# Interleaving TensorE transposes with products in a GLA and attention encoder

## The chip, the cores and the metric

The kernel runs on one core of one Trainium2 chip. The metric is the device time of one execution in microseconds (us); less is better. The executions shown below are of the kernel as it stood before the change.

## The reference

The reference is an encoder of two layers over 512 tokens of width 1024, in float32. Each layer is a token mixer and a gated MLP, each behind an RMS norm and with a residual:

```python
x = x + mixer(rmsnorm(x, norm_mix[i]))
x = x + conv_ffn(rmsnorm(x, norm_ffn[i]), ...)      # silu(gate) * val, width-3 convolution ahead
```

Layer 0 mixes by gated linear attention (GLA): 4 heads, keys of 128, values of 256 columns, chunks of 64, a scan in each direction. Its end is what the change touches:

```python
o = (o_f + o_b)                                     # per head: 512 tokens x 256
o = rmsnorm(o, norm_w) * silu(g)                    # the gated output
x = x + o.reshape(512, 1024) @ w_out
```

Layer 1 mixes by softmax attention: 8 query heads of 128, 2 key heads, 512 keys, swept in blocks of 128 queries:

```python
s = (q_blk @ k.T) * scale
p = softmax(s)                                      # 128 queries x 512 keys
o = p @ v                                           # then o.reshape(512, 1024) @ w_out
```

## The kernel before, in words

**Tiling.** Activations stand feature-major: 8 tiles of 128 features x 512 tokens. To keep float32's accuracy with operands of type `float32r`, every operand of a large product is split into a high part and a low part (what is left over), and one product becomes three matmuls into one accumulator: high by high, high by low, low by high (`mm3`, recorded at L350, L351, L352). A split takes one ScalarE copy (the high part) and one VectorE subtraction (the low part). Nearly every matmul moves 512 columns against a loaded 128x128 block.

**Stages.** In order: the GLA mixer (to about 205 us), MLP 0, attention (its block loop runs at about 628 to 727 us), MLP 1. Engines: PE does matmuls and transposes, DVE is VectorE, ACT is ScalarE, POOL is GpSimd; PEld are PE's weight loads. PSUM accumulators come from four pools of banks: `acc` 3, `s` 2, `pt` 2, `po` 1.

**Transposes.** Two results stand token-major and must be turned before they can be multiplied on. A transpose is a PE instruction on a 128x128 block, in groups of eight:
- `tail(h)` (L692 to L705) turns the gated output `gr` of GLA head `h`: for each of two column halves, four transposes into a `pt` bank (L699), then ACT copies it out with a scale as the high part of `oT` (L703) and DVE makes the low part (L704). Four heads, 32 transposes.
- `turn(h, i)` (L1094 to L1108) turns the probabilities of two query blocks: for each of two halves four transposes into a `pt` bank (L1105), then ACT (`pth`, L1107) and DVE (`ptl`, L1108). 16 calls, 128 transposes.

**GLA's heads.** Per head: scores inside the chunk (`inner`, L609), masked and split on ACT and DVE (`masked`: `at`, `ath`, `atl`, L616 to L622); state products (`kv`, `outer`), scanned on DVE into `sa` and `sb` (L655); the inner products with the values (L665) and with the states (`outputs`, L676). `gated(h)` then squares the output on ACT (L684), takes a power on POOL (L284), multiplies by the gate on DVE (L689, four instructions) and copies to `gr` by a DMA on POOL's queue (L690). `out_steps` (L408) is the output projection, cut into steps of six products; its first part works on the heads that are finished while the last head is still under way.

**Attention's loop.** Step `t` of the loop issues the scores of block `t` (three products, `s`), their maximum on DVE (`mx`, L1069), its scaling on ACT (`nb`, L1070), the exponential on ACT (`p`, L1072), and on DVE the reciprocal and the scaling (`rc`, L1077; `p`, L1078). ACT's queue then copies the block by DMA into a ring (L1090), from where it is turned five blocks later. `mix(h, k)` is the product with the values: three products per key block into the one `po` bank; after the fourth key block ACT and DVE split it into `oT` (L989, L990). The scores rotate over three banks. Query projections (`A`, `B`) and steps of the output projection (`op`) fill the rest of PE's time by two tables (`Q_STEPS`, `O_STEPS`).

**What sets the order.** The program is traced in Python; a scheduler then orders each engine's instructions by priority and by when it believes them ready, and adds the waits. Each engine issues its list strictly in that order. `with tc.issue_after(ins)` keeps what is traced inside it behind `ins` on the same engine. In the kernel before, attention's transposes and `mix` products have no such order; GLA's tails of heads 0 and 1 stand behind the head's last product:

```python
if h:
    tail(h - 1, last)                               # L744
with tc.issue_after(last.ins):
    last = qproj(h + 1, kqt)
```

and in attention, per step:

```python
for k in range(k, k + 1 if h < QH - 1 else NT):
    mix(h, k)                                       # L1141
if t >= LAG + 1 and (t - LAG) % 2 == 1 and t < len(blocks) + LAG:
    h, j = blocks[t - LAG]
    turn(h, j // 2)                                 # L1144
```

## Time and profile before

| | us |
|---|---|
| three executions | 1113.39, 1113.46, 1114.41 (median 1113.46) |
| profiled execution, its own time | 1113.35 |
| its span (first to last instruction) | 1111.6 |
| PE busy | 1104.1 (99%) |
| PE weight loads | 947.5 (85%) |
| DVE busy | 796.7 (72%) |
| ACT busy | 562.4 (51%) |
| POOL busy | 117.3 (11%) |
| granted TensorE clock | 0.999 |

The time contains 1.75 us outside the span. Matmuls are pipelined and their ends are modelled, so a product of 512 columns shows 0.39 us although products follow each other every 0.227 us; what a stretch costs PE is read from starts. A timeline row gives start, length, engine, line, operation, output <- inputs, shapes, count and, in brackets, the idle time before it with what ended it. A row with a count merges instructions that follow each other.

### The profile page before, as it was taken

To read this page: it belongs to the slowest core of one execution; us is meant where nothing else is said; L and a number is where in the kernel's file an instruction comes from. 1 tells how busy PE (TensorE), PEld (TensorE's weight loads), DVE (VectorE), ACT (ScalarE), POOL (GpSimd) and SP (SyncE) were. 2 spreads that over 40 slices of the span, in tenths; PEclk is the share of its full clock that TensorE was granted. 3 is DMA by queue.
4 is the path that set the end of the run, shared out by engine and by line. 5 is a ranking of instruction groups with operands and counts; after the bars stand their busy time and mean duration, and the time that the engine had idled before them with its cause. 6 is when DMAs were issued, how large, how long until landed. Compare 5 with 4: busy or idle time off the path is not lost.

```text
span 1111.6 us, 14744 instructions
## 1 busy us (share of the span) xinstructions
PE 1104.1 (99%) x5780; PEld 947.5 (85%) x5780; DVE 796.7 (72%) x1217; ACT 562.4 (51%) x870; POOL 117.3 (11%) x126
## 2 busy tenths in 40 slices
PE   9999999999999999999999999999999999999998
PEld 7888888888889988898888888788888998889887
DVE  6786784667889577975664588666788957797572
ACT  6565343444556444653464777644455644465340
POOL 0100122001001000100004333000100100010000
PEclk9999999999999999999999999999999999999999
DMA  6423122232226423363247665423222652336322
GB/s 230 152 76 112 59 95 77 76 114 76 76 88 177 155 76 113 102 165 114 97 130 186 174 191 161 143 76 108 82 76 82 172 164 76 114 96 167 117 76 76
DMA packets 31413, 130.52 MB, mean 117 GB/s; under 512 B 3824, under 2 KB 4336, under 8 KB 20976
## 3 DMA queue, kind: packets, MB, share of 16 engines
q1 hardware_dynamic: 21072, 102.16, 26.4%
q0 software_dynamic: 5376, 18.88, 8.5%
q10 hardware_dynamic: 4896, 8.55, 2.1%
q8 instruction: 45, 0.74, 0.3%
q14 instruction: 24, 0.20, 0.0%
HBM read 100.21 MB, written 2.10 MB: 92 GB/s over the span
## 4 chain that ended last, share of the span: by engine, by line
PE 96%; DVE 1%; issue 1%; ACT 1%; DMA 0%; POOL 0%; ACTq 0%; DVEq 0%; POOLq 0%
PE r L847 14%; PE up L350 14%; PE up L351 14%; PE up L352 14%; PE vg L382 8%; PE op L408 8%; PE dn L351 2%; PE dn L352 2%; PE dn L350 2%; PE A L350 1%; PE A L352 1%; PE A L351 1%; PE B L350 1%; PE B L351 1%; PE B L352 1%
## 5 line engine op out<-in xcount | busy, mean ns | idle before, releaser
L350 PE MATMUL up<-xhl,wh 128*128 128x512 f32 x704 | 274.4, 390 | 0.0
L351 PE MATMUL up<-xhl,wh 128*128 128x512 f32 x704 | 274.0, 389 | 0.0
L352 PE MATMUL up<-xhl,wl 128*128 128x512 f32 x704 | 273.9, 389 | 0.0
L199 ACT ACTIVATE wh<-raw 128x1024 fp32r<-128x1024 f32 x132 | 139.4, 1056 | 211.4 <-PE up L351 108.0
L200 DVE TENSOR_TENSOR wl<-raw,wh 128x1024 fp32r<-128x1024 f32 x132 | 161.1, 1220 | 41.2 <-ACT wh L199 40.9
L352 PEld LDWEIGHTS up<-xhl,wl 128*128 128x128 f32 x704 | 132.1, 188 | 27.5
L350 PEld LDWEIGHTS up<-xhl,wh 128*128 128x128 f32 x704 | 132.2, 188 | 27.1
L351 PEld LDWEIGHTS up<-xhl,wh 128*128 128x128 f32 x704 | 132.2, 188 | 27.0
L847 PE MATMUL r<-gu,wh 128*128 128x256 f32 x640 | 116.4, 282 | 0.0
L847 PEld LDWEIGHTS r<-gu,wh 128*128 128x128 f32 x640 | 99.7, 191 | 0.3
L789 DVE TENSOR_TENSOR u<-up,R 128x512 f32<-128x512 f32 x88 | 60.1, 685 | 54.0 <-PE up L352 54.0
L847 PE MATMUL r<-gu,wl 128*128 128x256 f32 x320 | 90.4, 283 | 0.0
L791 ACT ACTIVATE y<-u,cw 128x512 f32<-128x512 f32 x88 | 71.2, 811 | 33.1 <-DVE u L789 32.9
L382 PE MATMUL vg<-wh,xhl 128*128 128x512 f32 x256 | 79.7, 390 | 0.5 <-ACT sq L324 0.5
L408 PE MATMUL op<-oT,wh 128*128 128x512 f32 x256 | 71.8, 393 | 0.3 <-DVE g L689 0.3
L793 DVE SCALAR_TENSOR_TENSOR y<-u,cw,y 128x511 f32<-128x511 f32 x88 | 65.7, 748 | 2.0
L792 DVE SCALAR_TENSOR_TENSOR y<-u,cw,y 128x511 f32<-128x511 f32 x88 | 65.4, 744 | 1.2 <-ACT y L791 1.2
L795 ACT ACTIVATE y<-y 128x512 f32<-128x512 f32 x44 | 27.8, 633 | 72.0 <-DVE y L793 71.8
L847 PEld LDWEIGHTS r<-gu,wl 128*128 128x128 f32 x320 | 61.1, 191 | 0.0
L189 POOL DMA_DIRECT2D wl<-raw x32 | 28.1, 878 | 303.4 <-ACT wl L142 103.0
L382 PEld LDWEIGHTS vg<-wh,xhl 128*128 128x128 f32 x256 | 48.0, 188 | 10.6 <-ACT sq L324 0.7
L408 PEld LDWEIGHTS op<-oT,wh 128*128 128x128 f32 x256 | 47.3, 188 | 10.5 <-ACT oT L703 0.7
(232 smaller groups left out, 1928.3 us busy)
## 6 DMA issues: line engine op xcount, KB each, us to landing
raw<-in_w_up_dram SPq DMA_DIRECT2D x42, 1024.0 KB, 4.9
raw<-in_w_down_dram SPq DMA_DIRECT2D x22, 1024.0 KB, 4.8
wl<-raw POOLq DMA_DIRECT2D x32, 512.0 KB, 4.6
raw<-in_w_vg_dram SPq DMA_DIRECT2D x6, 1024.0 KB, 4.9
ring<-p ACTq DMA_DIRECT2D x22, 256.0 KB, 2.6
raw<-in_w_kq_dram SPq DMA_DIRECT2D x4, 1024.0 KB, 4.9
raw<-in_w_gout_dram SPq DMA_DIRECT2D x4, 1024.0 KB, 4.8
raw<-in_w_aout_dram SPq DMA_DIRECT2D x16, 256.0 KB, 4.5
```

Source lines behind the costliest of these rows:

```text
L199: act.activation(hi[:, sl], r[:, sl], AF.Copy)
L200: dve.tensor_tensor(lo[:, sl], r[:, sl], hi[:, sl].bitcast(F32), ALU.subtract)
L350: mm(ps, wh, mh, start=start, stop=False)
L351: mm(ps, wh, ml, start=False, stop=False)
L352: return mm(ps, wl, mh, start=False, stop=stop)
L382: mm(ps[j][:, :width], hl[k][i == 2][:, j * P : (j + 1) * P], (wl if i == 1 else wh)[:, sl], start=k == 0 and i == 0, stop=k == KC - 1 and ...
L408: mm(pss[ng][n], wt[:, sl], mv, start=k == 0 and i == 0, stop=k == KC - 1 and i == 2)
L789: dve.tensor_tensor(u, ps, norm.R, ALU.mult)
L791: act.activation(y, u, AF.Identity, scale=w(1), bias=w(3))
L792: dve.scalar_tensor_tensor(y[:, 1:], u[:, : S - 1], w(0), y[:, 1:], ALU.mult, ALU.add)
L793: dve.scalar_tensor_tensor(y[:, : S - 1], u[:, 1:], w(2), y[:, : S - 1], ALU.mult, ALU.add)
L847: mm(dst, w[:, sl], m, start=start and j == 0 and a == 0, stop=j == NQ - 1 and a == 2, skip_group_check=True)
```

## The change

Four edits; the products, the splits and the number of instructions stay.

1. `tail` and `turn` become generators that yield after two transposes and after each bank's copies. `behind` issues a PE instruction after the latest one of the same chain.
2. In GLA, the transposes of heads 0 and 1 are drawn between the steps (three products each) of the next head's query projection, those of heads 2 and 3 between the steps (six products) of the output projection. Its first part is now cut as four, two and two steps per column group instead of six and two, and from its third step on the products are chained in program order.
3. In the attention loop, `mix` yields after each of its three products, and each is chained; a pair of transposes is drawn ahead of each of them and ahead of its end. A step's chain starts behind the chain of the step before. The split of `po` is now traced behind the fourth pair.
4. For the last GLA head, `gated(2)` multiplies by the gate only after the low part `atl` of that head's masked scores.

```diff
--- before.py
+++ after.py
@@ -76,7 +76,18 @@
 ):
     nc = tc.nc
     pe, act, dve, pool, sync = nc.tensor, nc.scalar, nc.vector, nc.gpsimd, nc.sync
-    mm = pe.matmul
+    latest, chained = [None, None], [False]
+
+    def mm(*a, **k):
+        with tc.issue_after(latest[0].ins) if chained[0] else ExitStack():
+            latest[0] = pe.matmul(*a, **k)
+        return latest[0]
+
+    def behind(f, *a, **k):
+
+        with tc.issue_after(latest[0].ins) if latest[0] else ExitStack():
+            latest[0] = f(*a, **k)
+
 
     cp = ctx.enter_context(tc.tile_pool(name="cp", bufs=1))
     sp = ctx.enter_context(tc.tile_pool(name="sp", bufs=1))
@@ -554,9 +565,10 @@
                 pass
             return res
 
-        def qproj(h, kqt):
+        def qproj(h, kqt, beside=iter(())):
             psq = bank("acc" if h else "pt", "q")
-            last = feature_tile(*W.half(w_kq, 2 * h + 1), norm.hl, psq)
+            for last in feature_steps(*W.half(w_kq, 2 * h + 1), norm.hl, psq):
+                next(beside, None)
             dve.scalar_tensor_tensor(kqt[:, :S], psq, DK ** -0.5, norm.R, ALU.mult, ALU.mult)
             return last
 
@@ -619,8 +631,8 @@
             dve.copy_predicated(at3, msk, banks[1].rearrange("p (s c) -> p s c", c=P))
             hi, lo = f32r("u", "ath"), f32r("u", "atl")
             act.activation(hi, at, AF.Copy)
-            dve.tensor_tensor(lo, at, hi.bitcast(F32), ALU.subtract)
-            return hi, lo
+            on_dve = dve.tensor_tensor(lo, at, hi.bitcast(F32), ALU.subtract)
+            return hi, lo, on_dve
 
         def values(h):
 
@@ -676,7 +688,7 @@
                         last = mm(og[s], l, r, start=False, stop=i == len(parts) - 1, skip_group_check=True)
             return last
 
-        def gated(h, og):
+        def gated(h, og, after=None):
 
             oss = tiny(4, "oss")
             for s in range(NT):
@@ -686,23 +698,26 @@
             gr[h] = big(F32R, "gr")
             for s in range(NT):
                 r = g[s][:, h * DV : (h + 1) * DV]
-                dve.scalar_tensor_tensor(r, og[s], ors[:, s : s + 1], r, ALU.mult, ALU.mult)
+                with tc.issue_after(after.ins) if after else ExitStack():
+                    dve.scalar_tensor_tensor(r, og[s], ors[:, s : s + 1], r, ALU.mult, ALU.mult)
                 pool.dma_start(gr[h][:, s * DV : (s + 1) * DV].bitcast(F32), r)
 
-        def tail(h, last=None):
+        def tail(h):
 
             t3 = gr.pop(h)
             for c in range(2):
                 tp = bank("pt", "tp")
                 for s in range(NT):
-                    with tc.issue_after(last.ins) if last else ExitStack():
-                        pe.transpose(tp[:, s * P : (s + 1) * P].bitcast(F32R),
-                                     t3[:, s * DV + c * P : s * DV + (c + 1) * P], identr)
+                    behind(pe.transpose, tp[:, s * P : (s + 1) * P].bitcast(F32R),
+                           t3[:, s * DV + c * P : s * DV + (c + 1) * P], identr)
+                    if s == 1:
+                        yield
                 t = big(F32R, "oT") if h < 2 else pair("xhl", 8, F32R, "oT")
                 w = prm[:, PC_GN + c : PC_GN + c + 1]
                 act.activation(t[:, :S], tp, AF.Copy, scale=w)
                 dve.scalar_tensor_tensor(t[:, S:], tp, w, t[:, :S].bitcast(F32), ALU.mult, ALU.subtract)
                 oh[2 * h + c] = (t[:, :S], t[:, S:])
+                yield
 
         _, kqt = whole(kproj(0))
         ends, on_dve = keys(0, kqt)
@@ -733,7 +748,7 @@
                 last = outputs(h - 1, st, og, last)
                 banks, last = inner(h, last)
                 at = masked(banks)
-                gated(h - 1, og)
+                gated(h - 1, og, at[2])
             with tc.issue_after(on_act.ins) if h == 0 else ExitStack():
                 with tc.issue_after(on_dve.ins) if h == 0 else ExitStack():
                     vs = values(h)
@@ -741,19 +756,22 @@
             if h + 1 < GH:
                 with tc.issue_after(on_dve.ins):
                     ends, on_dve = keys(h + 1, kqt)
-                if h:
-                    tail(h - 1, last)
                 with tc.issue_after(last.ins):
-                    last = qproj(h + 1, kqt)
+                    last = qproj(h + 1, kqt, tail(h - 1) if h else iter(()))
         last = outputs(GH - 1, st, og, last)
         gated(GH - 1, og)
-        osteps = out_steps(w_gout, oh, nxt, (range(6), (6, 7)))
+        osteps = out_steps(w_gout, oh, nxt, (range(4), (4, 5), (6, 7)))
+        beside = iter(())
         for i in range(12):
-            if i == 4:
-                tail(GH - 2)
+            if i == 2:
+                beside = tail(GH - 2)
+            elif i == 8:
+                beside = tail(GH - 1)
+            next(beside, None)
+            chained[0] = i > 1
             next(osteps)
+        chained[0] = False
         sync.dma_start(cw, conv)
-        tail(GH - 1)
         for _ in osteps:
             pass
         return cw
@@ -1100,20 +1118,25 @@
             for c in range(2):
                 tp = bank("pt", "pt").rearrange("p (k q) -> p k q", q=2 * P)
                 for k in range(2):
+                    o = (2 * c + k) * P
                     for j in range(2):
-                        o = (2 * c + k) * P
-                        pe.transpose(tp[:, k, j * P : (j + 1) * P].bitcast(F32R), ps[j][:, o : o + P], identr)
+                        behind(pe.transpose, tp[:, k, j * P : (j + 1) * P].bitcast(F32R), ps[j][:, o : o + P], identr)
+                    if k == 0:
+                        yield
                 ph, pl = pts[h][c]
                 act.activation(ph[:, :, isl], tp, AF.Copy)
                 dve.tensor_tensor(pl[:, :, isl], tp, ph[:, :, isl].bitcast(F32), ALU.subtract)
+                yield
 
         def mix(h, k):
 
             if k == 0:
                 pos[h] = bank("po", "po")
             vo = k * 256 + (h // 4) * HD
-            ph, pl = pts[h][k // 2]
-            mm3(pos[h], vh[:, vo : vo + HD], vl[:, vo : vo + HD], ph[:, k % 2, :], pl[:, k % 2, :], k == 0, k == NT - 1)
+            v1, v2, (p1, p2) = vh[:, vo : vo + HD], vl[:, vo : vo + HD], (t[:, k % 2, :] for t in pts[h][k // 2])
+            for i, (a, b) in enumerate(((v1, p1), (v1, p2), (v2, p1))):
+                behind(mm, pos[h], a, b, start=k == 0 and i == 0, stop=k == NT - 1 and i == 2)
+                yield
             if k == NT - 1:
                 t = big(F32R, "oT") if h < 4 else pair("xhl", 8, F32R, "oT")
                 split(pos[h], t)
@@ -1133,15 +1156,23 @@
         for t in range(len(blocks) + LAG2):
             if t < len(blocks):
                 scores(*blocks[t])
-            for g in plan[t]:
-                next(g, None)
+            hosts = [g for g in plan[t]]
             if t >= LAG2 + NT - 1:
+                for g in hosts:
+                    next(g, None)
                 h, k = divmod(t - LAG2 - NT + 1, NT)
-                for k in range(k, k + 1 if h < QH - 1 else NT):
-                    mix(h, k)
+                hosts = [g for k in range(k, k + 1 if h < QH - 1 else NT) for g in [mix(h, k)] * 4]
+            turns = iter(())
             if t >= LAG + 1 and (t - LAG) % 2 == 1 and t < len(blocks) + LAG:
                 h, j = blocks[t - LAG]
-                turn(h, j // 2)
+                turns = turn(h, j // 2)
+            latest[0] = latest[1]
+            for g in hosts:
+                next(turns, None)
+                next(g, None)
+            for _ in turns:
+                pass
+            latest[1] = latest[0]
             if 1 <= t <= len(blocks):
                 copy(*blocks[t - 1])
             if t < len(blocks):
```

How the order moves, at three places.

DVE, GLA's last head: `atl` is the low part of the masked scores, the `g` rows are the gate of the head before, `sa` and `sb` the state's scan. Before:

```order
L619 COPY_PREDICATED at_1558<-smask,in_1553 128x512
L282 TENSOR_SCALAR ors_1574<-oss_1565 128x4
L689 SCALAR_TENSOR_TENSOR g_154<-o_1457,ors_1576,g_154 128x256
L689 SCALAR_TENSOR_TENSOR g_155<-o_1457,ors_1576,g_155 128x256
L622 TENSOR_TENSOR atl_1562<-at_1558,ath_1561 128x512
L689 SCALAR_TENSOR_TENSOR g_156<-o_1464,ors_1576,g_156 128x256
L689 SCALAR_TENSOR_TENSOR g_157<-o_1464,ors_1576,g_157 128x256
L655 SCALAR_TENSOR_TENSOR sa_1596<-sa_1596,fk_772,kv_1598 128x256
```

and now:

```order
L631 COPY_PREDICATED at_1558<-smask,in_1553 128x512
L293 TENSOR_SCALAR ors_1574<-oss_1565 128x4
L667 SCALAR_TENSOR_TENSOR sa_1596<-sa_1596,fk_772,kv_1598 128x256
L634 TENSOR_TENSOR atl_1562<-at_1558,ath_1561 128x512
L702 SCALAR_TENSOR_TENSOR g_154<-o_1457,ors_1576,g_154 128x256
L702 SCALAR_TENSOR_TENSOR g_155<-o_1457,ors_1576,g_155 128x256
L702 SCALAR_TENSOR_TENSOR g_156<-o_1464,ors_1576,g_156 128x256
L702 SCALAR_TENSOR_TENSOR g_157<-o_1464,ors_1576,g_157 128x256
L667 SCALAR_TENSOR_TENSOR sb_1597<-sa_1596,fk_772,kv_1599 128x256
```

The gate's four multiplications stood around `atl`; they now stand behind it, and one scan step has come ahead of it.

PE, attention, the steps in which head 4 begins (`s` scores, `po` values' product, `pt` transposes, `op` output projection). Before:

```order
L1105 MATMUL pt_6248<-ident,ring_5343 128x128 x4
L1105 MATMUL pt_6255<-ident,ring_5343 128x128 x4
L350 MATMUL s_6266<-k_5176,q_6212 128x512
L351 MATMUL s_6266<-k_5176,q_6212 128x512
L352 MATMUL s_6266<-k_5176,q_6212 128x512
L408 MATMUL op_6099<-oT_6245,wh_5916 128x512
L408 MATMUL op_6100<-oT_6245,wh_5916 128x512
L350 MATMUL po_6278<-pth_6179,vh_5333 128x512
```

and now, from the same transposes on (lines 83 and 89 are the wrapper and the chain of the new file):

```order
L89 MATMUL pt_6242<-ident,ring_5343 128x128 x2
L83 MATMUL po_6148<-pth_6025,vh_5333 128x512
L89 MATMUL pt_6242<-ident,ring_5343 128x128 x2
L83 MATMUL po_6148<-ptl_6026,vh_5333 128x512
L89 MATMUL pt_6251<-ident,ring_5343 128x128 x2
L83 MATMUL po_6148<-pth_6025,vl_5334 128x512
L89 MATMUL pt_6251<-ident,ring_5343 128x128 x2
L83 MATMUL s_6222<-k_5176,q_6212 128x512 x2
L83 MATMUL s_6266<-k_5176,q_6212 128x512 x2
L83 MATMUL s_6222<-k_5176,q_6212 128x512
L83 MATMUL s_6266<-k_5176,q_6212 128x512
L83 MATMUL s_6285<-k_5176,q_6212 128x512 x3
L83 MATMUL op_6099<-oT_6259,wh_5916 128x512
L83 MATMUL op_6100<-oT_6259,wh_5916 128x512
L83 MATMUL s_6324<-k_5176,q_6212 128x512
L83 MATMUL po_6278<-pth_6176,vh_5333 128x512
```

The eight transposes, which followed each other, now stand in pairs with a `po` product between them; behind them come the scores of four blocks with two `op` products among them, where before one block's scores, two `op` products and the next head's first `po` product came.

PE, one turn of the next step. Before:

```order
L350 MATMUL po_6278<-pth_6179,vh_5333 128x512
L351 MATMUL po_6278<-ptl_6180,vh_5333 128x512
L352 MATMUL po_6278<-pth_6179,vl_5334 128x512
L1105 MATMUL pt_6307<-ident,ring_5343 128x128 x4
L1105 MATMUL pt_6314<-ident,ring_5343 128x128 x4
L408 MATMUL op_6099<-oT_6245,wl_5917 128x512
L408 MATMUL op_6100<-oT_6245,wl_5917 128x512
```

and now:

```order
L83 MATMUL po_6278<-pth_6176,vh_5333 128x512
L83 MATMUL po_6278<-ptl_6177,vh_5333 128x512
L83 MATMUL po_6278<-pth_6176,vl_5334 128x512
L89 MATMUL pt_6304<-ident,ring_5343 128x128 x2
L83 MATMUL po_6278<-pth_6176,vh_5333 128x512
L89 MATMUL pt_6304<-ident,ring_5343 128x128 x2
L83 MATMUL po_6278<-ptl_6177,vh_5333 128x512
L89 MATMUL pt_6313<-ident,ring_5343 128x128 x2
L83 MATMUL po_6278<-pth_6176,vl_5334 128x512
L89 MATMUL pt_6313<-ident,ring_5343 128x128 x2
L83 MATMUL s_6324<-k_5176,q_6212 128x512 x2
L83 MATMUL op_6099<-oT_6259,wh_5916 128x512
```

Three `po` products that stood ahead of the transposes now stand between their pairs.

Counted over PE's whole list, attention's 128 transposes stood in 18 unbroken runs before and stand in 62 now; GLA's 32 stood in 4 and stand in 16.

## The prediction

> **What bounds the kernel now.** I read the page first, then PE's waits, then a table by stretch, then the timeline where PE waits or transposes.
>
> ```profile
> span 1111.6 us, 14744 instructions
> PE 1104.1 (99%) x5780; PEld 947.5 (85%) x5780; DVE 796.7 (72%) x1217; ACT 562.4 (51%) x870; POOL 117.3 (11%) x126
> PE 96%; DVE 1%; issue 1%; ACT 1%; DMA 0%; POOL 0%; ACTq 0%; DVEq 0%; POOLq 0%
> ...
> 628.00:725.00 97.00, 95.23 (x503) 78.70 (x503) 73.19 (x149) 68.84 (x151) 26.69 (x22) 1.00 0.56 166
> 695.00:705.00 10.00, 8.48 (x45) 6.41 (x45) 7.62 (x17) 8.46 (x19) 0.00 (x0) 1.00 0.27 103
> ```
>
> The second and third rows say that PE bounds it: busy for 99% of the span, 96% of the chain that ended last. So an edit is worth what it changes in PE's own time, and the waits it takes from or gives to PE. The two rows by stretch (columns: PE, PE loads, DVE, ACT, POOL busy, granted clock, DMA share) are attention's loop: PE is idle for 1.8 of 97 us, and 1.5 of that lies between 695 and 705, where ACT is busy for 8.5 of 10. There is little to win, and I first ask what a transpose costs.
>
> ```profile
> 649.55 0.39 PE L351 MATMUL po<-ptl,vh 128*128 128x512 f32 x1
> 649.78 0.40 PE L352 MATMUL po<-pth,vl 128*128 128x512 f32 x1
> 650.01 0.80 PE L1105 MATMUL pt<-ident,pr 128*128 128x128 f32 x8
> 650.65 0.47 PE L350 MATMUL s<-k,q 128*128 128x512 f32 x1
> 650.96 0.40 PE L351 MATMUL s<-k,q 128*128 128x512 f32 x1
> ...
> 698.94 0.39 PE L352 MATMUL po<-pth,vl 128*128 128x512 f32 x1
> 699.17 0.46 PE L1105 MATMUL pt<-ident,pr 128*128 128x128 f32 x4
> 699.47 0.46 PE L350 MATMUL s<-k,q 128*128 128x512 f32 x1
> 699.77 0.40 PE L351 MATMUL s<-k,q 128*128 128x512 f32 x1
> ```
>
> From the product ahead of a group to the second product behind it lie two products and the group. For eight: 650.96 - 649.78 = 1.18 us, less two products of 0.227 (649.55 to 649.78) leaves 0.725. For four: 699.77 - 698.94 = 0.83, less 0.455 leaves 0.375. So one more transpose costs (0.725 - 0.375) / 4 = 0.0875 us, and a group costs about 0.03 whatever its size. That last part shows in the first product behind: it lasts 0.47 instead of 0.39 and its successor starts 0.31 after it instead of 0.227. A load that a product of 0.227 hides sticks out from behind a transpose.
>
> **The change part by part.** *Pairs.* The trace has no pair. By the two sizes one costs 0.03 + 2 x 0.0875 = 0.205, and four pairs 0.82 instead of 0.725: every further cut costs 0.03. Attention's transposes go from 18 runs to 62: 44 x 0.03 = 1.3 us. GLA's go from 4 to 16: 0.36. Bounds: if a pair costs what the starts of a group's first transposes suggest (rival one below), it is 0.12; if it pays a start 0.06 later, a step of 0.0875 and the full 0.083 by which the product behind is late, it is 0.23, and all twenty groups together lose 20 x 4 x (0.23 - 0.205) = 2.0 us more. I take 0.205, since groups of four and of eight give the same step.
>
> [...]
>
> *GLA's last head.* The next rows are PE, then ACT, then DVE.
>
> ```profile
> 175.13 0.64 PE L665 MATMUL o<-vr,ath 128*128 128x256 f32 x4
> 176.12 0.50 PE L408 MATMUL op<-oT,wh 128*128 128x512 f32 x1 [0.35 <-DVE g L689]
> 176.72 0.39 PE L665 MATMUL o<-vr,atl 128*128 128x256 f32 x1
> ...
> 173.90 0.39 ACT L653 ACTIVATE sa<-kv 128x256 f32<-128x256 f32 x1 [0.44 <-PE kv L352]
> 174.18 0.62 ACT L621 ACTIVATE ath<-at 128x512 fp32r<-128x512 f32 x1
> ...
> 175.19 0.88 DVE L689 SCALAR_TENSOR_TENSOR g<-o,ors,g 128x256 f32<-128x256 f32 x2 [1.15 <-POOL ors L284]
> 175.98 0.68 DVE L622 TENSOR_TENSOR atl<-at,ath 128x512 fp32r<-128x512 f32 x1
> 177.37 0.47 DVE L655 SCALAR_TENSOR_TENSOR sa<-sa,fk,kv 128x256 f32<-128x256 f32 x1
> ```
>
> From 175.13 to 176.72 PE issues four products of 0.12 (0.64 less the last one's 0.28, over three) and one of 0.227, 0.71 us of work in 1.59: 0.88 is waiting, for `atl`, which is queued behind two gate instructions. `ath` is there at 174.80. In the new order one scan step (0.47) comes first, possible from 174.29, so `atl` runs from 174.80 to 175.48, and PE asks for it after three products at 175.49: some 0.05 remains. Gain 0.8. What is late next: the gate, behind `atl`, ends at 175.48 + 4 x 0.44 = 177.2 instead of about 177.4, so nothing. The three scan steps left then end at 177.2 + 3 x 0.47 = 178.6, before it was four from 177.37, 179.3: 0.7 earlier, for a PE that comes 0.8 earlier.
>
> *GLA's tails.* PE also waits behind the transposes of heads 2 and 3, for ACT's and DVE's copies:
>
> ```profile
> 187.22 0.40 PE L408 MATMUL op<-oT,wl 128*128 128x512 f32 x1
> 187.49 0.73 PE L408 MATMUL op<-oT,wh 128*128 128x512 f32 x2
> 197.99 1.34 PE L408 MATMUL op<-oT,wh 128*128 128x512 f32 x4
> ```
>
> 187.22 to 187.49 is 0.04 over 0.227, the pair of 0.73 is 0.11 over 0.62, and the four are 0.19 over 0.31 + 2 x 0.227 + 0.39. With pairs ahead of steps of six products (1.36 us), `oT` has more than two steps, 2.7 us, from its last pair to its use, where now PE asks for it a few products behind the group and only 0.15 to 0.19 is missing. Gain 0.3. GLA: -0.8 - 0.3 + 0.36 = **-0.75**.
>
> *Attention.* The waits of its loop:
>
> ```profile
> 679.12 1.08 PE L1105 MATMUL pt<-ident,ring 128*128 128x128 f32 x8
> ...
> 700.00 0.40 PE L352 MATMUL s<-k,q 128*128 128x512 f32 x1
> 701.14 0.53 PE L1105 MATMUL pt<-ident,pr 128*128 128x128 f32 x4 [0.74 <-DVE ptl L1108]
> 702.01 0.50 PE L350 MATMUL s<-k,q 128*128 128x512 f32 x1 [0.34 <-ACT p L1072]
> 703.88 0.47 PE L350 MATMUL po<-pth,vh 128*128 128x512 f32 x1 [0.44 <-DVE oT L990]
> ...
> 699.11 0.20 ACT L1072 ACTIVATION_READ_ACCUMULATOR p<-s,nb,qsc 128x1 f32 x1
> 699.34 0.16 DVE L1077 RECIPROCAL rc<-sm 128x1 f32<-128x1 f32 x1 [0.55 <-ACT p L1072]
> 699.42 0.67 DVE L1069 TENSOR_REDUCE mx<-s 128x1 f32<-128x512 f32 x1
> 700.01 0.47 DVE L1078 TENSOR_SCALAR p<-p,rc 128x512 f32<-128x512 f32 x1
> 700.13 0.30 ACT L1070 ACTIVATE nb<-mx,qsc 128x1 f32<-128x1 f32 x1 [0.33 <-DVE mx L1069]
> 700.52 0.47 ACTq L1090 DMA_DIRECT2D ring<-p  x1
> 701.09 0.78 ACT L1072 ACTIVATE p<-s,nb,qsc 128x512 f32<-128x512 f32 x1 [0.67 <-DVE ptl L1108]
> ```
>
> At 679 the eight last 1.08 instead of 0.80; as at 701.14, where the row names DVE's `ptl`, I take it that a bank wasn't free. Pairs come slower, so this 0.28 goes. Between 700 and 704 PE waits 0.91 (701.14 less 700.00 and 0.227), 0.57 (702.01 less 701.14, over the 0.30 that four take at 699.17) and 0.6 (three scores and two `op` products from 702.01 would end at 703.23). These 2.06 stand on the last rows: ACT's exponential ends at 699.31, then DVE's reciprocal, maximum and scaling, then the copy's issue on ACT's queue, then the next exponential at 701.09. That cycle turns once in about 2.65 us per block, and none of its parts is changed. Where PE has less than that to do per block, it waits, in whichever place; there the cuts of three groups (9 x 0.03 = 0.3) hide too. So attention: +1.3 - 0.3 - 0.28 = **+0.7**.
>
> Sum: 1113.35 - 0.75 + 0.7 = 1113.3 on the profiled execution, whose time lies 0.11 under the median of three. I predict **1113.4**; alone, from cuts that are free to the dear pair, this case spans 1112.0 to 1115.4. A measurement can tell about 0.2% from no change, 2.2 us: below 1111.2 is faster, above 1115.7 slower.
>
> **The rivals.** *One: both loads of a pair are hidden.*
>
> ```profile
> 650.01 0.23 PE L1105 MATMUL pt<-ident,pr 128*128 128x128 f32 x1
> 650.01 0.29 PE L1105 MATMUL pt<-ident,pr 128*128 128x128 f32 x2
> 650.01 0.37 PE L1105 MATMUL pt<-ident,pr 128*128 128x128 f32 x3
> ```
>
> These are the first one, two and three of a group, seen through ever longer windows: the second ends 0.06 after the first and the third 0.08 after that, so that two start with less than a step of 0.0875 between them. If the early starts are work and not only issue, a pair costs 0.12, a group 0.49 instead of 0.725, twenty groups gain 4.7 us instead of losing 1.7, and the time is 1113.46 - 0.8 - 0.3 - 0.28 - 4.7 = 1107.4. Against it: the product behind is late by the same 0.083 after four as after eight, so the lag is handed on, not gone. [...] Chance 0.08.
>
> *Two: attention's waits go too.* Spread copies and a chained order could let the cycle run ahead, so that the 2.06 us at 700 to 704 vanish while all cuts are paid: 1113.4 + 0.3 - 2.06 = 1111.6. For it: `pth` for the second bank started at 699.21, 2.5 us after its transposes, behind other work of ACT that the new order partly moves. Against: the cycle's rows. Chance 0.14, a third of it below 1111.2.
>
> *Three: clumps of scores block the chain.* Where head 4 begins the new list has the scores of three blocks, two `op` products and the fourth block's first score in a row, so that this one is due 11 x 0.227 = 2.5 us after the clump begins; but there are three banks. It must wait until the first block's exponential is done: 0.68 of scores, 0.67 maximum, 0.30 and 0.98 on ACT, 2.6 us, which just fits if the cycle is idle. If it is one block behind, PE stands for a turn, 2.65 us, and the first `po` product and the pairs are queued behind the waiting score. That gives 1113.4 + 2.65 = 1116.1 for one clump. For it: PE already waited for `p` at 702.01. Against: the products after it are work that PE then has in stock, and would give back part. Chance 0.22.
>
> **How the numbers follow.** Forecast 0.56, rivals 0.08, 0.14, 0.22. Faster: 0.08 and 0.05 of rival two, 0.13. Slower: rival three and 0.02 of the forecast's upper end, 0.24. Within 0.2%: 0.63. The range leaves out rival one and a second clump: 1110.9 to 1116.4.
>
> **What would show it.** In the changed profile a product behind a pair should be followed after about 0.31 us, and a pair should take 0.205; PE's weight loads and counts stay. At 175 us the 0.88 wait should shrink to under 0.1, and no wait should stand behind GLA's last transposes. At 679 no wait inside a turn. Between 695 and 705 PE should still wait about 2 us. The forecast is wrong if pairs measure 0.12, if the loop from 628 to 727 shortens by more than 1 us, or if a score waits for `p` over 1 us ahead of a chained `po` product.

## The result: 0.6% slower

| | before | after |
|---|---|---|
| median of four executions each, on one chip | 1113.93 us | 1120.91 us |
| all | 1113.39 to 1116.06 | 1120.73 to 1121.84 |
| profiled execution, its own time | 1113.35 | 1121.84 |

The ratio is 1.0061, with a 95% interval of 1.0043 to 1.0078: the change makes the kernel slower by some 7 us. The prediction was 1113.4, no change that could be measured, within 1110.9 to 1116.4. It was wrong.

The page of the kernel after, its span and its busy times:

```profile
span 1120.1 us, 14739 instructions
PE 1108.6 (99%) x5780; PEld 947.7 (85%) x5780; DVE 800.1 (71%) x1217; ACT 564.5 (50%) x870; POOL 117.6 (10%) x126
```

The counts of each engine are the same. PE's busy time grew by 4.5 us and the span by 8.5, so some 4 us are open idle time of PE; of the 4.5, part is cost of cuts and part is time in which PE was busy at half its clock, as will be seen. Where the 8.5 us arise is read from three products that mark the stages: MLP 0's first `up`, attention's first score `s`, MLP 1's first `up`. First PE's timeline of before, then of after (start, length, engine, line, operation, output <- inputs, shapes, count):

```profile
225.48 0.39 PE L350 MATMUL up<-xhl,wh 128*128 128x512 f32 x1
...
616.70 0.40 PE L350 MATMUL s<-k,q 128*128 128x512 f32 x1
...
754.17 0.39 PE L350 MATMUL up<-xhl,wh 128*128 128x512 f32 x1
```

```profile
229.25 0.62 PE L83 MATMUL up<-xhl,wh 128*128 128x512 f32 x2
...
620.47 0.86 PE L83 MATMUL s<-k,q 128*128 128x512 f32 x3
...
762.66 0.61 PE L83 MATMUL up<-xhl,wh 128*128 128x512 f32 x2
```

GLA ends 3.77 us later. MLP 0 adds nothing: the first score is late by the same 3.77. Attention's loop takes 762.66 - 620.47 = 142.19 instead of 137.47, 4.72 more, and MLP 1 adds nothing again. So 3.77 + 4.72 = 8.49, which is the difference of the two profiled executions. The profiled execution of after is the slowest of its four, 0.9 us above their median, and the only one whose granted clock reads 0.998 and not 1.000; the profiled one of before is 0.6 under its median. So the medians differ by 7.0 and not by 8.5. There are two losses, in two places.

**The price of a pair** is not one of them. PE's timeline of after, in attention:

```profile
668.36 0.29 PE L89 MATMUL pt<-ident,ring 128*128 128x128 f32 x2
668.49 0.47 PE L83 MATMUL po<-pth,vh 128*128 128x512 f32 x1
668.79 0.29 PE L89 MATMUL pt<-ident,ring 128*128 128x128 f32 x2
```

A pair and a product take 668.79 - 668.36 = 0.43, so a pair takes 0.20 beside a product of 0.227.

**GLA.** The last head's low part no longer makes PE wait (from 175.61 three products of 0.12, then the first with `atl`: 0.09 of waiting where 0.88 was):

```profile
175.61 0.52 PE L83 MATMUL o<-vr,ath 128*128 128x256 f32 x3
176.06 0.38 PE L83 MATMUL o<-vr,atl 128*128 128x256 f32 x1
```

The loss comes 6 us later. PE's timeline of after, then DVE's gate of head 3, then two rows of the table by stretch (PE, PE loads, DVE, ACT, POOL busy with counts, then the granted clock, DMA share, GB/s):

```profile
182.13 0.63 PE L83 MATMUL op<-oT,wl 128*128 128x512 f32 x2
185.03 0.36 PE L89 MATMUL tp<-ident,gr 128*128 128x128 f32 x2 [2.28 <-DVE g L702]
185.23 1.16 PE L83 MATMUL op<-oT,wh 128*128 128x512 f32 x4
186.23 0.92 PE L83 MATMUL op<-oT,wl 128*128 128x512 f32 x2
186.95 0.42 PE L89 MATMUL tp<-ident,gr 128*128 128x128 f32 x2
187.17 2.04 PE L83 MATMUL op<-oT,wh 128*128 128x512 f32 x4
189.00 0.99 PE L83 MATMUL op<-oT,wl 128*128 128x512 f32 x2
189.83 0.29 PE L89 MATMUL tp<-ident,gr 128*128 128x128 f32 x2
...
184.10 1.66 DVE L702 SCALAR_TENSOR_TENSOR g<-o,ors,g 128x256 f32<-128x256 f32 x4 [1.16 <-POOL ors L295]
...
186.00:188.00 2.00, 2.00 (x8) 1.56 (x7) 0.00 (x0) 0.59 (x1) 1.33 (x3) 0.59 0.59 197
188.00:190.00 2.00, 2.00 (x8) 1.44 (x7) 0.75 (x1) 0.85 (x2) 0.00 (x0) 0.55 0.19 66
```

Head 2's first pair is due at 182.13 + 2 x 0.227 = 182.58 and starts at 185.03: 2.45 us of waiting. The row names DVE's gate `g`. That is not head 2's own gate, which DVE did from 175.92 to 177.57; it is head 3's, the DVE row here. The code says why: `outer` puts the last head's outputs into the `pt` banks (`bank("pt" if h == GH - 1 else "s", "o")`), there are two of them, and a tail's target `tp` is a `pt` bank too. A bank is free only when head 3's gate has read it, during 184.10 to 185.76. Before, the tail stood 24 products into the projection and met the bank just free; the change draws it after 12, and the products behind it are chained, so nothing can pass. After the wait the granted clock falls, to 0.59 over 186 to 188 and 0.55 over 188 to 190, which is 3.4 us at half clock in all (0.41 and 0.45 of 2 us each, doubled). The six products from 187.17 to the next pair take 2.66 us instead of 1.44, and the pair at 186.95 starts 0.27 late. That pair goes to the same bank as the first one, so it waits for no other bank: the product ahead of it is already at half clock. So +2.45 for the wait and +1.49 for the clock, less 0.79 for `atl`, less 0.3 for the copies PE no longer waits for, plus 0.36 for cuts: 3.2 of the 3.77. Of the rest, 0.23 stands already at 99 us, ahead of every edit, and 0.3 is not accounted for.

**Attention.** PE's timeline of after, at its five longest waits:

```profile
634.09 1.52 PE L83 MATMUL s<-k,q 128*128 128x512 f32 x6
636.39 1.05 PE L83 MATMUL hs<-bd,qa 128*128 128x2 f32 x8 [0.77 <-DVE qa L973]
...
646.82 0.46 PE L89 MATMUL pt<-ident,ring 128*128 128x128 f32 x4
647.95 0.50 PE L83 MATMUL s<-k,q 128*128 128x512 f32 x1 [0.68 <-DVE q L1008]
...
697.29 2.81 PE L83 MATMUL s<-k,q 128*128 128x512 f32 x9
700.72 0.73 PE L83 MATMUL op<-oT,wh 128*128 128x512 f32 x2 [0.62 <-ACT oT L1007]
...
708.53 0.70 PE L83 MATMUL s<-k,q 128*128 128x512 f32 x2
710.29 0.97 PE L83 MATMUL s<-k,q 128*128 128x512 f32 x3 [1.06 <-ACT p L1090]
711.27 0.73 PE L83 MATMUL op<-oT,wh 128*128 128x512 f32 x2
712.67 0.51 PE L83 MATMUL po<-pth,vh 128*128 128x512 f32 x1 [0.67 <-DVE oT L1008]
```

By starts: six scores end their turn at 634.09 + 6 x 0.227 = 635.45, `hs` comes at 636.39, 0.94 late. Four transposes take 0.30 to the next product, so 647.95 is 0.83 late. Nine scores behind transposes would be over at 697.29 + 2.13 = 699.42, so `op` is 1.30 late. Two scores from 708.53 leave 710.29 1.22 late, and two products from 711.27 leave 712.67 0.95 late. That is 5.2 us, where before the loop had 2.3 (2.06 at 700 to 704 and 0.28 at 679); the rest is small delays, above all some 0.1 at each product behind a wait, which shows 0.50 instead of 0.39. Cuts, 44 x 0.03 = 1.3, and waits, 3.4, make the 4.72.

Why `oT` is late at 700.72 is seen on ACT's timeline of after:

```profile
697.74 0.58 ACT L1127 ACTIVATE pth<-pt 128x512 fp32r<-128x512 f32 x1
...
698.97 0.59 ACT L1127 ACTIVATE pth<-pt 128x512 fp32r<-128x512 f32 x1
699.89 0.30 ACT L1088 ACTIVATE nb<-mx,qsc 128x1 f32<-128x1 f32 x1 [0.33 <-DVE mx L1087]
700.09 0.58 ACT L1007 ACTIVATE oT<-po 128x512 fp32r<-128x512 f32 x1
```

The last `po` product stands ahead of the nine scores, at 696.73. Its copy `oT` is taken up at 700.09, behind both copies of a turn, `pth`, the exponential between them and the next block's `nb`; it is now traced behind the copies. In these rows ACT keeps to its list: it stands idle for 0.33 us ahead of `nb` at 699.89, though the input of `oT` has been there since about 697.2 (696.73 and the 0.47 that the product shows).

### The profile page after: what moved, and what is told of

The parts are those of the page before. It is cut to its first block, busy times and chain, and to the rows that moved or that the text cites. A ratio compares the mean times of both kernels' runs of the same rounds, so it can differ in the third digit from the quotient of the medians.

```text
span 1120.1 us, 14739 instructions
## 1 busy us (share of the span) xinstructions
PE 1108.6 (99%) x5780; PEld 947.7 (85%) x5780; DVE 800.1 (71%) x1217; ACT 564.5 (50%) x870; POOL 117.6 (10%) x126
## 4 chain that ended last, share of the span: by engine, by line
PE 81%; DVE 2%; ACT 1%; issue 0%; ACTq 0%; DVEq 0%
PE up L83 43%; PE r L83 14%; PE op L83 8%; PE dn L83 6%; PE A L83 2%; PE B L83 2%; PE po L83 2%; PE s L83 2%; PE av L83 1%; PE pt L89 1%; DVE mx L1087 0%; PE hs L83 0%; ACT p L1090 0%; DVE p L1096 0%; DVE ptl L1128 0%
## 5 line engine op out<-in xcount | busy, mean ns | idle before, releaser
L83 PE MATMUL up<-xhl,wh 128*128 128x512 f32 x1408 | 434.1, 389 | 0.0
L83 PE MATMUL dn<-gu,wh 128*128 128x512 f32 x192 | 59.1, 389 | 0.0
L820 ACT ACTIVATE gu<-y 128x512 fp32r<-128x512 f32 (+1 forms) x60 | 34.5, 575 | 38.4 <-DVE y L814 17.6
```

The lines of the kernel that those rows point to most:

```text
L83: latest[0] = pe.matmul(*a, **k)
L820: act.activation(t[:, o : o + n], y, AF.Copy)
```

## The experiments: GLA

All runs were timed in five rounds beside the kernel before, on one chip for each group; differences of medians are against that kernel's own median in the same group (1113.76 to 1114.13). An interval of a ratio is some 0.1% to each side, 1 us.

**Only edit 4.** On the kernel before:

```diff
-                gated(h - 1, og)
+                gated(h - 1, og, at[2])
```

> Only edit 4 on the kernel before: the gate of GLA head 2 stands behind atl. The prediction gave this edit 0.8 us, and the changed kernel's marks agree (kv of the last head later by 0.48, its last o product earlier by 0.31). Theory: 0.8 us faster than before, all of it gone by the last o product near 180.5 us. Rival: the gain is only lent; the scan steps and the gate of the last head, all on DVE, are later by as much and PE waits for them in the output projection. Then 0.0.

Measured: 1113.34 against 1113.89, 0.55 less; ratio 0.9996 (0.9987 to 1.0004). The interval holds both the theory's 0.8 and zero. In its profile `atl` costs no wait (as in the rows of after). But a part of the gain is only lent, as the rival has it for all of it. PE's timeline of this kernel shows head 2's eight transposes:

```profile
185.37 1.02 PE L700 MATMUL tp<-ident,gr 128*128 128x128 f32 x8
```

The next product starts at 186.23, 0.86 behind their start; before it was 0.63 (186.06 to 186.69). PE comes to the turn earlier, and the turn's second bank is still read by the gate of the last head, which DVE does from 184.15 to 185.81. So 0.2 of the 0.8 is given back at a `pt` bank; the size of the whole is not settled by the time.

**GLA's edits alone,** with attention's loop as before:

> All of GLA's edits (1, 2 and 4), attention's loop as before. Theory: GLA's part of the change loses 3.8 us by itself, as the mark at MLP 0's start in the changed kernel says (3.77), and nothing downstream gives it back: 3.8 us slower than before. Rival, the prediction's own account: 0.75 us faster. Rival two: half of the 3.8 is given back in MLP 0 or attention, so under 2 us slower.

Measured: 1116.98 against 1113.89, 3.1 slower; ratio 1.0023 (1.0013 to 1.0032). The theory holds; nothing is given back later. The ten times stand in two groups, three at 1115.56 to 1115.62 and seven at 1116.81 to 1117.21. The granted clock of each execution tells them apart: 1.000 in the three, 0.998 in the seven, of which the profiled one is one. So the clock falls in some executions of this kernel and not in others, and the fall costs 1.5 us between the medians of the groups, as in the rows of after.

**The bank taken away.** Order, cuts and chain stay; only the target of head 2's first four transposes is another bank:

```diff
-                tp = bank("pt", "tp")
+                tp = bank("po" if h == GH - 2 and c == 0 else "pt", "tp")
```

> As the run with GLA's edits alone, but the first four transposes of head 2 go to the po bank, which nothing else holds then, and not to a pt bank that still holds the last head's outputs; order and cuts stay. Theory (the bank): the wait of 2.67 us at 182.4 and the low clock behind it vanish, about 4 us less than with GLA's edits alone, so 0.2 to 0.8 us faster than before. Rival (the cuts or the chain themselves cost it): the time stays over 2 us above before.

Measured: 1113.43 against 1113.89, 0.5 less; ratio 0.9995 (0.9986 to 1.0004). PE's timeline and a stretch of this kernel:

```profile
182.74 0.62 PE L83 MATMUL op<-oT,wl 128*128 128x512 f32 x2
183.21 0.29 PE L89 MATMUL tp<-ident,gr 128*128 128x128 f32 x2
...
186.00:188.00 2.00, 2.00 (x12) 1.56 (x11) 1.84 (x3) 1.06 (x1) 1.94 (x4) 1.00 0.39 131
```

The pair follows the products without a gap and the clock stays 1.00. One word of the program, `po` for `pt`, is worth 3.5 us. This shows the bank as the cause of the whole GLA loss, the low clock included.

**One step later.** GLA's edits alone, the tail of head 2 drawn at the projection's fourth step, not its third:

```diff
-            if i == 2:
+            if i == 3:
```

> As the run with GLA's edits alone, but head 2's transposes are drawn one step of six products later, so PE has 1.36 us more to do before it must wait for the bank: a wait of about 1.1 us instead of 2.45. Theory (the clock falls only behind the long wait, as the granted clock stays 1.00 through attention's waits of up to 1.24 us): no low clock, so the wait alone is left over the run with the po bank, -0.46 + 1.1 = 0.6 us slower than before. Rival (any wait over 1 us at this place is followed by some 3 us at half the clock): 2.0 us slower.

Measured: 1114.65 against 1113.94, 0.7 slower; ratio 1.0006 (0.9998 to 1.0015).

```profile
183.63 0.61 PE L83 MATMUL op<-oT,wl 128*128 128x512 f32 x2
185.15 0.36 PE L89 MATMUL tp<-ident,gr 128*128 128x128 f32 x2 [0.91 <-DVE g L702]
...
186.00:188.00 2.00, 2.00 (x12) 1.60 (x11) 0.36 (x1) 1.45 (x2) 1.45 (x3) 1.00 0.58 197
```

The wait is 185.15 - 183.63 - 0.454 = 1.07 and the clock behind it stays at 1.00: 2.3 us less than with GLA's edits alone, for 1.4 us less of waiting. The granted clock is 0.999 or 1.000 in all eleven executions. The fall of the clock is a price of the long wait, not of the place.

## The experiments: attention

For each kernel the loop's length is taken from the starts of its first score and of MLP 1's first product, as above; it is free of what GLA's stage does. Its cuts are the runs of transposes in the list less the 18 of before, at 0.03 each, and what is left is waits; in the rows with +8.06 and +20.69 it also holds time at half clock, as will be seen.

| kernel | first `s` to MLP 1 | over before (137.47) | cuts | waits | median over before |
|---|---|---|---|---|---|
| edit 3 alone, 62 runs | 617.01 to 759.26 | +4.78 | 1.3 | 3.5 | +4.55 |
| fours, 31 runs | 617.54 to 757.47 | +2.46 | 0.4 | 2.1 | +2.42 |
| eights, 19 runs | 616.60 to 756.16 | +2.09 | 0.0 | 2.1 | +1.79 |
| split early, 63 runs | 616.91 to 757.75 | +3.37 | 1.35 | 2.0 | +2.89 |
| fours and split early, 31 runs | 616.62 to 756.58 | +2.49 | 0.4 | 2.1 | +2.41 |
| no chain, 52 runs | 617.32 to 758.04 | +3.25 | 1.0 | 2.2 | +3.16 |
| pairs, scores in order, 61 runs | 617.07 to 758.88 | +4.34 | 1.3 | 3.0 | +5.96 |
| fours, scores in order, 30 runs | 617.03 to 762.56 | +8.06 | 0.4 | 7.7 | +8.16 |
| eights, everything in order, 16 runs | 616.34 to 774.50 | +20.69 | -0.1 | 20.8 | +21.31 |

**Edit 3 alone:**

> Only edit 3: attention's turns and mix as in the changed kernel, GLA as before. Theory: the parts add, so 4.7 us slower than before: 1.3 for 44 more cuts, 3.3 for more waits. Rival: attention's waits come from where GLA's delay left its loads; then about 1.3 to 2 us slower.

Measured: 1118.44 against 1113.89; ratio 1.0044 (1.0031 to 1.0057). Its waits are those of the kernel after, at the same products. The two parts' losses, 3.1 and 4.55, add up to 7.65 where the whole change has 7.0, the same within the intervals; the clock fell in seven of the ten executions of GLA's edits alone and in one of the four of the whole change.

**Fours:** a bank's transposes drawn together.

```diff
-                    if k == 0:
-                        yield
```

> As the run with attention's edit alone (4.55 us slower than before), but a bank's four transposes are drawn together, so the 128 stand in 31 runs, not 62; chain and everything else stay, and nine scores in a row are left. Theory (cuts and waits are two separate costs): 31 x 0.03 = 0.93 less, 3.6 us slower than before. Rival (the cuts are the cause, and the waits only show them): under 1.5 us slower. Rival two (the cuts hide in the waits): 4.5 us slower, as with pairs.

Measured: 1116.55 against 1114.13; ratio 1.0021 (1.0012 to 1.0030). It is 1.2 better than the theory had it: beside 0.9 of cuts, 1.4 of waits are gone. Pairs cost more than their own time.

**The split of `po` ahead of the last copies:**

```diff
-                yield
-            if k == NT - 1:
-                t = big(F32R, "oT") if h < 4 else pair("xhl", 8, F32R, "oT")
-                split(pos[h], t)
-                oh[h] = (t[:, :S], t[:, S:])
+                if k == NT - 1 and i == 2:
+                    t = big(F32R, "oT") if h < 4 else pair("xhl", 8, F32R, "oT")
+                    split(pos[h], t)
+                    oh[h] = (t[:, :S], t[:, S:])
+                yield
```

> As the run with attention's edit alone, but the split of po into oT is written right behind the last product of a head, ahead of the last pair of transposes and the copies of their bank. Theory (the split behind both copies makes oT late): the waits of op and po for oT, 0.79 and 0.84 us over a product's 0.227, go, so some 3 us slower than before. Rival (those waits are the block's cycle of exponential, scaling and copy, met elsewhere): PE waits for p or ptl instead and the time stays 4.5 us above before.

Measured: 1117.02 against 1114.13; ratio 1.0027 (1.0016 to 1.0038), near the theory's 3. PE's timeline:

```profile
696.10 0.61 PE L83 MATMUL op<-oT,wh 128*128 128x512 f32 x2
697.10 0.50 PE L83 MATMUL po<-pth,vh 128*128 128x512 f32 x1 [0.38 <-DVE oT L1001]
```

`op` no longer waits for ACT's `oT`; the `po` product behind it now waits for DVE's half, by 0.55 (697.10 less 696.10 and 0.45). The later `po` product, which was 0.95 late in the kernel after, is still 0.5 late. The score's wait for `p` stays.

**Both mends:**

> Attention's edit with both mends: a bank's four transposes drawn together and the split of po ahead of the last copies. Alone the two took 2.1 and 1.7 us off the 4.55. Theory (different causes): they add up to 3.7, so some 0.9 us slower than before, with PE still waiting for p once, about 1 us near 705. Rival (both shorten the same late copies, so the second gives little): 2 us slower or more.

Measured: 1116.35 against 1113.94; ratio 1.0022 (1.0013 to 1.0030). The rival holds: with fours the early split gives nothing. Both mends take away the same 1.4 us, and 2.1 of waits stay.

**No chain:** the same generators, nothing held behind its forerunner.

```diff
-                        behind(pe.transpose, tp[:, k, j * P : (j + 1) * P].bitcast(F32R), ps[j][:, o : o + P], identr)
+                        pe.transpose(tp[:, k, j * P : (j + 1) * P].bitcast(F32R), ps[j][:, o : o + P], identr)
...
-                behind(mm, pos[h], a, b, start=k == 0 and i == 0, stop=k == NT - 1 and i == 2)
+                mm(pos[h], a, b, start=k == 0 and i == 0, stop=k == NT - 1 and i == 2)
```

> As the run with attention's edit alone, but nothing is chained: pairs are still written between the products of mix, and the scheduler is free to order them. It puts the first eight transposes in a row ahead of hs again, makes 52 runs of the 128, and leaves nine scores in a row. Theory (the chain moves transposes out of the places where they covered waits): the first wait, 0.93 us for qa, goes, 0.3 of cuts goes, and the waits near 700 partly remain: 2 to 3.3 us slower than before. Rival (spread pairs wait by themselves, with or without a chain): 4.2 us or more slower.

Measured: 1117.29 against 1114.13; ratio 1.0028 (1.0017 to 1.0039), within the theory's 2 to 3.3. The wait of `hs` is gone, but others took its place. PE's waits, grouped (for, by, total, times, longest):

```profile
PE pt L1116 <- DVE ptl L1121: 0.9, 2, 0.5
PE pt L1116 <- PE s L83: 0.5, 1, 0.5
```

Now transposes stand at PE's head and wait for a `pt` bank, or for what has to read it. So the theory has its number, but not its reason: leaving out the chain saved ten cuts (0.3 us) and one wait, and 2.2 of waits are there all the same.

**Scores in program order, with pairs and with fours.** In all lists above nine scores (with the early split and pairs, seven) stand in a row where head 4 begins, as rival three had it. Here the scores are put into the chain too, three at a time:

```diff
+            latest[0], chained[0] = latest[1], bool(latest[1])
             if t < len(blocks):
                 scores(*blocks[t])
+            latest[1], chained[0] = latest[0] if latest[1] else None, False
```

> As the run with attention's edit alone (pairs; 4.55 us slower than before), but from the loop's third key block on the scores too stand in program order, in the chain of mix and turns: no six or nine scores in a row any more, three at a time. Theory (clumps of scores, which outrun the chained products, make the waits near 700 us): the 3.3 us of waits over a product's time from 694 to 710 shrink to the 2 that the kernel before has there, or less; 2.5 to 3.3 us slower than before. Rival (the chained turns' late copies of p make them, whatever the scores do): 4.2 us or more slower.

> The same with a bank's four transposes drawn together (2.4 us slower than before without it). Theory of the clumps: 0.5 to 1.4 us slower than before, and the waits of op for oT and of s for p, 0.85 and 0.83, are gone. Rival (late copies): 2.2 us or more slower.

Measured: 1119.72 (profiled execution 1118.08) and 1121.92 against 1113.76; ratios 1.0050 (1.0036 to 1.0063) and 1.0076 (1.0064 to 1.0089). The theory of clumps fell: without a clump the waits are 3.0 with pairs, not 2 or less, and 7.7 with fours, of which up to 1.7 are half clock (3.4 us of it, around the second row below). The score's wait for `p` is gone in both, but others have grown, that of `hs` from 0.77 to 1.45 with pairs. The late copies of `p` aren't shown by it either, since the longest wait with fours is that of two `op` products, drawn straight behind scores, for `oT`:

```profile
709.62 0.73 PE L83 MATMUL op<-oT,wh 128*128 128x512 f32 x2 [2.03 <-ACT oT L1000]
...
712.00:714.00 2.00, 2.00 (x6) 1.55 (x5) 0.69 (x1) 0.29 (x1) 0.00 (x0) 0.50 0.87 293
```

**Eights in the chain:** a turn drawn in one go, ahead of mix's first product.

```diff
-                    if k == 0:
-                        yield
                 ph, pl = pts[h][c]
                 act.activation(ph[:, :, isl], tp, AF.Copy)
                 dve.tensor_tensor(pl[:, :, isl], tp, ph[:, :, isl].bitcast(F32), ALU.subtract)
-                yield
+            yield
```

> As the run with attention's edit alone, but a turn's eight transposes are drawn in one go ahead of mix's first product: 19 runs of transposes instead of 62, no product between them; the chain over the step, and nine scores in a row, stay. Theory (the chain makes the waits, by holding a step's products behind a transposed block whose copies or inputs are late): cuts cost nothing, the waits stay, 2 to 2.5 us slower than before. Rival (spreading the transposes makes the waits, since their copies come later): within 0.7 us of before.

Measured: 1115.66 against 1113.87; ratio 1.0017 (1.0008 to 1.0026), a little under the theory's 2 to 2.5 by the times and within it by the loop. With nothing cut or spread, 2.1 us of waits are there. Where one of them is from is seen on ACT and DVE of this kernel, then on ACT of before:

```profile
694.41 0.29 ACT L1081 ACTIVATE nb<-mx,qsc 128x1 f32<-128x1 f32 x1 [1.11 <-DVE mx L1080]
694.61 0.58 ACT L1000 ACTIVATE oT<-po 128x512 fp32r<-128x512 f32 x1
...
693.68 0.69 DVE L1080 TENSOR_REDUCE mx<-s 128x1 f32<-128x512 f32 x1 [0.68 <-PE s L83]
```

```profile
691.79 0.60 ACT L989 ACTIVATE oT<-po 128x512 fp32r<-128x512 f32 x1 [0.58 <-PE po L352]
692.29 0.28 ACT L1070 ACTIVATE nb<-mx,qsc 128x1 f32<-128x1 f32 x1
```

Before, ACT takes `oT` as soon as `po` is there and then the next block's `nb`. In the chained list `nb` stands ahead of `oT`. It waits 1.11 us with ACT idle, for the maximum of a score that PE issues only behind that same `po` (last `po` product at 692.10, the nine scores from 692.33), and `oT` waits with it. PE's next products are `op`; they start at 695.24, 0.87 after the nine scores' turn.

**Versions meant to beat both.** The kernel with GLA's edits and the `po` bank, and attention as before but for the projection's steps (27 moved to 28; 24 and 27 moved to 26 and 28):

> A version meant to beat both: GLA's edits with head 2's first four transposes in the po bank (0.46 us faster than before), attention as before, but the output projection's fourth step is drawn at step 28 of the loop, not 27, so that PE has two of its products more after 697 us, where it waits 2.06 us for the block's cycle. Theory: each product that is moved into those waits is saved from where it stood: 0.5 to 1 us faster than before. Rival: where it stood PE has nothing else and waits as much: 0.4 us faster, as without it.

> Again a version meant to beat both: GLA's edits with the po bank, attention as before, but the third and fourth steps of its output projection are drawn at steps 26 and 28 of the loop, not 24 and 27. The list of PE is then another one behind 690 us: four op products stand behind the last clump of three scores, and single scores nearer to the cycle's pace. Theory: 0.7 to 1 us of the 2.06 us of waits at 700 is filled, so 1.1 to 1.5 us faster than before. Rival: the products are taken from a place where they filled a wait as well, so 0.5 us faster, as without it.

Measured: 1113.43 against 1114.13, ratio 0.9993 (0.9984 to 1.0002), and 1117.14 against 1113.94, ratio 1.0027 (1.0018 to 1.0036). The first moved two products behind three scores and three products of mix, and left PE's waits near 700 us as they were: by its profile, in which the loop is 137.48 us long, its rival holds. The second filled those waits in part, and a turn's second transpose met a block that wasn't yet in the ring:

```profile
711.99 0.46 PE L1123 MATMUL pt<-ident,ring 128*128 128x128 f32 x3 [2.38 <-DMA ring<-p]
```

Seven of its ten executions have a granted clock of 0.997 or 0.998, at 1116.65 to 1119.15; the three at 1.000, the profiled one among them, took 1115.41 to 1115.79. So about half of the 3.2 us comes with the low clock.

The last version holds all of the loop in program order, with uncut turns:

> A version meant to beat both: GLA's edits with head 2's first four transposes in the po bank, and attention with whole turns of eight as before, but its scores, products and transposes all kept in program order: three scores at a time, never more. Theory of the clumps: the waits near 700 (2.06 us) go for the most part, so 1 to 2.5 us faster than before. Rival (the block's cycle of 2.65 us sets the pace there in any order): 0.5 us faster, as without it.

Measured: 1135.07 against 1113.76; ratio 1.0190 (1.0176 to 1.0204), 21 us slower. Each query head's `hs` now stands right behind the scores, and PE waits for its input:

```profile
656.81 1.87 PE L83 MATMUL hs<-bd,qa 128*128 128x2 f32 x8 [2.71 <-DVE qa L973]
```

Two such waits bring 6.8 us at half clock each, which is up to 6.8 of the loop's 20.7; the rest is waits. So a scheduler that lets scores and projections run ahead is worth some 20 us to this loop, and in no run did a more fixed order pay. Of all kernels, edit 4 alone, GLA's edits with the `po` bank and the latter with a moved step have medians 0.46 to 0.70 below before, but each interval reaches past 1, so that none is shown to be faster.

## Why the prediction was wrong

**The price of a pair: right.** 0.205 was predicted, 0.20 measured, and the 1.3 us for attention's cuts with it: fours cost 0.4 over eights in the loop (139.93 less 139.56), as 12 x 0.03 has it. Rival one, cheap pairs, is out. Cuts that are free, from which the prediction had its 1112.0, are shown by no run: what the runs showed is 0.03 for each.

**GLA's last head: right.** The wait fell from 0.88 to 0.09. The gain of 0.8 is in the profile; with edit 4 alone 0.2 of it is given back, and the time, 0.55 less, can't tell the rest from nothing. It is given back where the next step failed: at a `pt` bank that the last head's gate still reads.

**GLA's tails: wrong, by 4 us in the profiled execution, 2.5 of them the wait.** The step that failed is "no wait should stand behind GLA's last transposes" and the gain of 0.3 with it. It looked at what waits *behind* the transposes (copies of `oT`) and never asked what the transposes themselves wait for when they start 12 products earlier. The prediction named banks for attention and didn't look up whose bank `tp` takes here. The input `gr` was early; the output's bank was not free. With another bank the sum for GLA, -0.75, is met within what a time can tell (-0.5).

**The clock: not foreseen.** 1.5 us of GLA's loss, in the executions that have it, is the lower clock after the wait. A wait was priced as its own length.

**Attention: wrong, by 4 us.** The step that failed is "+1.3 - 0.3 - 0.28": it let the waits at 700 to 704 stay at 2.06 and hide cuts. The runs show 3.5 more of waits instead. Of these, 1.4 come with pairs and go with either mend, drawing fours or splitting `po` earlier: the split now stood behind a turn's last copies. The other 2.1 are there with uncut eights as well. Two causes of these are seen in rows, not taken away by a run of their own: the eight transposes that stood ahead of `hs` at 632 us now stand behind it, so that `hs` asks for `qa` 0.94 too early; and `oT` is behind `nb` on ACT. What the prediction should have done is to follow ACT's and DVE's lists too, and not PE's alone.

**Rival three came nearest.** It named the clump where head 4 begins, a score that must wait for `p`, and chained products queued behind it, with 1116.1 for one clump and a chance of 0.22. That wait is there (1.06 in its row at 710.29), and it goes where the clump goes; but the loss doesn't go with it: with scores in program order the waits are 3.0 instead of 3.5 with pairs, and far more with fours. Rival two, the cycle running ahead, is out.

**The range** was too narrow because both open terms, a wait for a bank in GLA and waits in attention's chain, had been set to nothing rather than bounded. "What is late next" was asked of the gate and the scans, not of every instruction that was moved forward.

What stays open: how the 2.1 us of waits would go in the new order. Freed from the chain they were 2.2, at other instructions; why both are so near each other isn't settled. All kernels of the table but the last have one more thing in common that no run tells apart: a turn is traced ahead of or between the products of mix, where before it was traced behind them. No kernel here put a chained turn behind mix and left the scores free, and none put `oT` ahead of `nb` and changed nothing else.

## What to carry to other kernels

When an instruction is moved forward, look first at what its output overwrites: find who still reads that bank and when the read ends, before counting what its input or its followers gain. When work on an engine that is the bound is spread or chained, follow the lists of the engines that evict its results; a copy that is traced one step later may stand behind a whole turn of another cycle, as `oT` did at 700.09. And where the engine is busy for 99% of the time, cutting runs has a price (here 0.03 us a cut) and nothing to fill, so name the idle time that a new order is to fill before paying for it.

## What was unexpected of the hardware

**PE's clock after a wait.** Products of 512 columns, 0.227 apart in the rows at full clock, came 0.427 apart for some time after some waits (188.15 to 188.57 in the kernel after), and the granted clock read 0.50 in a whole stretch (the row above of 712 to 714). This followed waits of 2.03 (`op` at 709.62), 2.28 (`tp` at 185.03) and 2.71 us (`hs` at 656.81), by the idle time in their rows. It did not follow waits of 0.91 (`tp` of the run one step later) and 1.06 us (attention's `s` at 710.29), nor the 2.38 us before 711.99 in the second version meant to beat both, whose next stretch is at 1.00:

```profile
712.00:714.00 2.00, 2.00 (x13) 1.75 (x14) 1.69 (x5) 1.76 (x6) 0.00 (x0) 1.00 0.35 133
```

So one wait of 2.03 us was followed by half clock and one of 2.38 was not, and even in one kernel the clock falls in some executions and not in others (seven of ten with GLA's edits alone).

The half clock also begins at different times after the waits. In the kernel after it begins at 186.37, 1.3 us behind the wait's end, and lasts 3.41 us, to 189.78 (the two rows from 186 to 190 miss 0.41 and 0.45 of 2 us each, at half clock). With GLA's edits alone it begins 0.3 us behind the wait's end and lasts 3.4; with fours and scores in order 1.5 us behind, for 3.4; in the version all in program order 0.4 and 0.5 us ahead of the ends of two waits, for 6.8 each. So the beginning isn't set by the wait's end alone, and the lengths are 3.4 or twice that.

The clock record of the profile gives the lengths more finely. In the kernel after the half clock lasts 3.413 us, and the full clock 180.906 ahead of it and 931.839 behind it, 53.0 and 273.0 times as long; in that of before the full clock lasts 1105.918, 324.0 times as long. In the 3.41 us right ahead of these three falls PE is busy for 1.34 (182.96 to 186.37 in after), for 1.31 (1106.80 to 1110.21 in before, where PE's work ends) and not at all (1118.21 to 1121.62 in after, behind PE's last product). No fall follows 1114.80 to 1118.21 in after, with 1.80 busy, or 700.62 to 704.03 in before, with 2.11. The author's estimate from these numbers is that it matters how a wait's idle time lies against such stretches of 3.41 us; two profiles don't settle that, and no run moved a wait to test it.
